# Moving the last of seven block products behind the next pair's second one, and three repeated weight loads some steps later

## The chip, the cores and the metric

One Trainium2 chip, one of its cores. The metric is device time in microseconds (us) of one execution of the whole kernel, taken as the median over runs. Engines are named as the profile names them: PE is TensorE, DVE is VectorE, ACT is ScalarE, POOL is GpSimd, SP is SyncE, which here issues DMAs.

## The reference, cut to what matters

The kernel computes one encoder layer over 1024 tokens of width 1024. A normed input goes through one combined projection into windowed attention, a two-way RWKV-7 scan and gates; their sum is projected and added to `x`. Behind that come the two steps that the change touches, and a gated embedding:

```python
hf = rms_norm(x, norm_ffn[i])
x = x + jnp.square(jax.nn.relu(hf @ w_ff1[i])) @ w_ff2[i]
hp = rms_norm(x, norm_ple[i])
x = x + (p[i] @ w_ple[i]) * jax.nn.sigmoid(hp @ w_ple_gate[i])
```

`w_ff1` is 1024 x 4096 and `w_ff2` 4096 x 1024, all in 32-bit floats. `hf @ w_ff1` is called the first MLP product here, the product with `w_ff2` the second.

## The kernel before, in words

Every operand of a matmul is split in two: ACT casts it to a rounded high part (line 187), DVE or POOL subtracts to get the low part (line 188). A product of two operands is then three matmuls, high x high, high x low and low x high, accumulated in a PSUM bank.

Both MLP products are done as 2 x 2 blocks with seven block products instead of eight, the sums and differences of blocks being formed on DVE.

**First MLP product** (lines 1300 to 1555). The 4096 hidden columns are 32 blocks of 128; pair `p` of 16 (`NPR`) takes blocks `p` and `p + 16`. Its raw weights come in two loads of 512 KB, one for each block (`w1_load`, line 1315), into the tile `w1st`, which has one buffer. From them `w1_op(p, r)` makes the operand of block product `r`: for S1 to S4 first sums on DVE (lines 1324 to 1331, tile `ssum`), then the split into `w1h` and `w1l`. Each of the seven operands has one buffer of its own, so `w1_op(p + 1, r)` must wait for product `r` of pair `p`. The right-hand sides are the normed tokens and their sums, made once: `fh`/`fl` (for A11 and A12), `rh`/`rl` (S2 and S4), `T1`, `T3` and `T4` (S1, S3, A22).

`product` (line 1442) is one block product: 12 matmuls of 128x512 into one bank of a pool of six (`ff1ps`). A pair takes three banks. `pa` gets A11 and then A12 on top; `pb` gets S2, then S3, then A22; `pc_` gets S1, then S4. Between them the partial sums are read out: line 1475 copies A11 (`c1`), line 1518 adds `c1` and `pb` after S2 (`u2`), line 1522 copies `pc_` after S1 (`c5`), line 1531 adds `c1` and `pb` after S3 (`u3`), line 1537 adds after S4, line 1547 after A22. Since S3 and A22 are added to what stands in `pb`, each must wait until the read before it is done. `relu2` squares the positive part, on ACT (lines 1457 and 1458) or, for A12's result, on DVE (line 1460). `hsum` (line 1465) forms the sums that the second product needs, and `put` (line 1469) stores the seven hidden blocks of a pair to DRAM, 256 KB each.

The loop of line 1495 runs over pairs. It is written in the order A11, S2, S1, A12, S3, S4, A22, and behind each product `then(r)` prepares the same operand of the next pair. The load for the pair after the next is written at the end. Pairs 0 and 1 have their A11 and A12 done ahead of the loop, and are interleaved in part.

**Second MLP product** (lines 1560 to 1720). Seven block products again (`PRODS`), each of 16 steps `p`; a step takes one hidden block (`hid_d`, tile `sst`, left side, split into `sh` and `sl`) and one block of `w_ff2` or a sum of such blocks (split into `th` and `tl`), and does 12 matmuls into four banks. B11's 16 blocks are kept raw in `b11`, since later products need them for sums. In the first block product, steps 0 to 2 (`NPRE`) take operands that were loaded and split during the first MLP product (`pre`); for these B11 is loaded a second time, into `b11` (line 1681). Steps 3 and on load B11 into `b11` (line 1606) and split it from there. From step 8 on (`T1EARLY` is 8) `t1_of(0)`, `t1_of(1)` and so on form T1 = B12 - B11 beside the products; they are the first to read the repeated blocks.

A scheduler orders the instructions of each engine, by dependencies and priority, at build time; each engine then runs its own in that order. SP's DMAs are one such queue: an issue that waits for a buffer holds up the issues behind it.

Of the kernel before, what the change touches and what calls it, by code (L numbers as in the profile page):

```python
# [12 lines left out]
ALU = mybir.AluOpType  # L13
# [124 lines left out]
def block_kernel(ctx: ExitStack, tc: tile.TileContext, I: dict, out: bass.AP):  # L138
    nc = tc.nc

    def pool(stack, name, bufs=1, **kw):
        return stack.enter_context(tc.tile_pool(name=name, bufs=bufs, reuse_waits="tile", **kw))
# [333 lines left out]
    with ExitStack() as s1:  # L476
# [75 lines left out]
        s2 = A1.tile([P, 2, 512], F32R, name="s2")  # L552
# [61 lines left out]
        for p in range(NP):  # L614
# [24 lines left out]
            for d in range(ND):  # L639
# [8 lines left out]
                if d == 0:  # L648
                    nc.vector.memset(E[:, :, 0:1], 1.0)
                    E1, E2, last = E[:, :, 0:C], E[:, :, 1:C + 1], C - 1  # L650
                else:
                    nc.vector.memset(E[:, :, C:C + 1], 1.0)
                    E1, E2, last = E[:, :, 1:C + 1], E[:, :, 0:C], 0
# [151 lines left out]
    with ExitStack() as s2:  # L805
# [16 lines left out]
        for n in range(NT):  # L822
# [6 lines left out]
            for kv in range(2):  # L829
# [6 lines left out]
                for h in range(4):  # L836
                    sc = PA.tile([P, nk * P], F32, name="sc", tag="sc", bufs=2)
                    for j in range(2):
                        nc.tensor.matmul(sc, qT[:, 4 * kv + h, :], kT[:, kv, j, k0 * P:k1 * P], start=(j == 0), stop=(j == 1))
                    nc.vector.tensor_tensor_reduce(  # L840
                        out=sm[:, h, 0:nk * P], in0=sc, in1=band[:, b0:b0 + nk, :].rearrange("p b t -> p (b t)"), scale=1.0,
# [460 lines left out]
    NPR = FF // P // 2  # L1302
# [136 lines left out]
    def bank():  # L1439
        return PG.tile([P, 512], F32, name="ff1ps", tag="w", bufs=6)  # L1440

    def product(ps, p, r, start=True):

        ah, al = wop[p, r]
        bh, bl = right[SUMS[r]]
        for k in range(4):
            for i, (x_, y_) in enumerate(((ah, bh), (ah, bl), (al, bh))):
                nc.tensor.matmul(ps, x_[:, k, :], y_[:, k, :], start=start and k + i == 0, stop=k == 3 and i == 2, skip_group_check=True)  # L1448

    def tmp(name, bufs=1):  # L1450
        return FP.tile([P, 512], F32, name=name, bufs=bufs)

    def relu2(src_, on_act):

        h = tmp("h", 7)
        if on_act:
            nc.scalar.activation(out=h, in_=src_, func=AF.Relu)  # L1457
            nc.scalar.activation(out=h, in_=h, func=AF.Square)  # L1458
        else:
            nc.vector.scalar_tensor_tensor(out=h, in0=src_, scalar=0.0, in1=src_, op0=ALU.max, op1=ALU.mult)  # L1460
        return h

    def hsum(a_, b_, op):
        h = tmp("h", 7)
        nc.vector.tensor_tensor(out=h, in0=a_, in1=b_, op=op)  # L1465
        return h

    def put(p, r, h):
        nc.sync.dma_start(hid_d[r][p], h)
# [8 lines left out]
    for p in range(2):  # L1478
        pa, pb = bank(), bank()
# [12 lines left out]
    sFP = ExitStack()  # L1492
    FP = pool(sFP, "post", side="right")
    sRF = ExitStack()
    for p in range(NPR):
        def then(r):

            if p + 1 < NPR:
                w1_op(p + 1, r)

        if p == 1:
            w1_op(2, "A11")
            w1_op(2, "A12")
        if p > 1:
            pa = bank()
            product(pa, p, "A11")
            c1_of(p, pa)
            then("A11")
        else:
            s_ = tmp("u2")  # L1510
            nc.vector.tensor_tensor(out=s_, in0=c1s[p], in1=first[p], op=ALU.add)
            a11 = relu2(s_, True)
            put(p, "A11", a11)
        pb, pc_ = bank(), bank()
        c1 = c1s[p]
        product(pb, p, "S2")
        u2 = tmp("u2")
        nc.vector.tensor_tensor(out=u2, in0=c1, in1=pb, op=ALU.add)
        then("S2")
        product(pc_, p, "S1")  # L1520
        c5 = tmp("c5")
        nc.scalar.copy(c5, pc_)
        then("S1")
        if p > 1:
            product(pa, p, "A12", start=False)
            a11 = relu2(pa, True)
            put(p, "A11", a11)
            then("A12")
        product(pb, p, "S3", start=False)
        u3 = tmp("u3")  # L1530
        nc.vector.tensor_tensor(out=u3, in0=c1, in1=pb, op=ALU.add)
        nc.vector.tensor_tensor(out=c5, in0=c5, in1=u3, op=ALU.add)
        a22 = relu2(c5, True)
        put(p, "A22", a22)
        then("S3")
        product(pc_, p, "S4", start=False)
        nc.vector.tensor_tensor(out=u2, in0=u2, in1=pc_, op=ALU.add)
        a21 = relu2(u2, True)
        s1 = hsum(a21, a22, ALU.add)
        put(p, "S1", s1)  # L1540
        s2 = hsum(s1, a11, ALU.subtract)
        put(p, "S2", s2)
        put(p, "S3", hsum(a11, a21, ALU.subtract))
        then("S4")
        product(pb, p, "A22", start=False)
        u3 = tmp("u3")
        nc.vector.tensor_tensor(out=u3, in0=c1, in1=pb, op=ALU.add)
        a12 = relu2(u3, False)
        put(p, "A12", a12)
        put(p, "S4", hsum(a12, s2, ALU.subtract))  # L1550
        then("A22")
        if p + 2 < NPR:
            w1_load(p + 2)
        if p == NPR - 2:
            RF = pool(sRF, "ff2a", bufs=1, side="right")
# [6 lines left out]
    NPRE, NR2, T1EARLY = 3, 5, 8  # L1562

    def w2_block(p, b):
        f, n = p + NPR * (int(b[1]) - 1), int(b[2]) - 1
        return w2[f * P:(f + 1) * P, 512 * n:512 * n + 512]
# [23 lines left out]
    b11 = pool(sB11, "b11").tile([P, NPR, 512], F32, name="b11r")  # L1590
# [84 lines left out]
    for ip, (lr_, rr_, bs, fresh) in enumerate(PRODS):  # L1675
        if fresh:
            banks[bs] = [acc() for _ in range(4)]
        for p in range(NPR):
            if ip == 0 and p < NPRE:
                sh, sl, th_, tl_ = pre[p]  # L1680
                nc.sync.dma_start(b11[:, p], w2_block(p, "B11"))
            else:
                sh, sl = parts_of(F2, ("sh", "sl"), fetch(F2, hid_d[lr_][p], "sst", 3), NR2)
                th_, tl_ = parts_of(F2, ("th", "tl"), right_of(p, rr_), NR2)
            for i in range(4):
                isl = slice(i * P, (i + 1) * P)
                for j, (x_, y_) in enumerate(((sh, th_), (sh, tl_), (sl, th_))):
                    nc.tensor.matmul(banks[bs][i], x_[:, isl], y_, start=fresh and p + j == 0,  # L1688
                                     stop=p == NPR - 1 and j == 2, skip_group_check=True)
            if ip == 0 and p == NPRE - 1:  # L1690
                sRF.close()
                sFP.close()
                PXX = pool(sX, "x1", side="right")
                X = [PXX.tile([P, 4, DM], F32, name=f"X{e}") for e in range(2)]
                c1 = pool(sC1, "c1", side="right").tile([P, 4, 512], F32, name="c1r")
                t2r = pool(sT2, "t2", side="right").tile([P, NPR, 512], F32, name="t2r")
                t1r = pool(sT1, "t1", side="right").tile([P, NPR, 512], F32, name="t1r")
            if ip == 0 and p >= NPR - T1EARLY:
                t1_of(p - (NPR - T1EARLY))
            if ip == 1 and p % 2 == 0:  # L1700
                e, i = divmod(p // 2, 4)
                t = torder[4 * e + i]
                nc.sync.dma_start(X[e][:, i, :], x1_d[t * P:(t + 1) * P, :])
            if ip == 3 and p < 12:
                add_to(*((0, 1), (1, 1), (1, 0))[p // 4], p % 4, c1[:, p % 4])
            if ip > 3 and p % 3 == 1:
                load_next()
            if ip == 6:
                if p == 4:
                    pt, xs = ple_load(0), ple_norm(0)  # L1710
                    ple_scale(0, *xs)
                if p == 9:
                    nxt = [ple_p(pt), ple_x(xs[0])]
        for i in range(4):
            b_ = banks[bs][i]
            if ip == 0:
                nc.scalar.copy(c1[:, i], b_)
            else:
                for e, n in {1: [(0, 1)], 2: [(0, 0)], 3: [(1, 1)], 4: [(1, 1)], 5: [(1, 0)], 6: [(0, 1)]}[ip]:
                    add_to(e, n, i, b_)  # L1720
        if ip == 3:
            sB11.close()
            PLEW = pool(sP, "plew")
            gainp = PLEW.tile([P, DM], F32, name="gainp", bufs=1)
            nc.sync.dma_start(gainp, I["gains"][2:3, :].partition_broadcast(P))
            wp = [PLEW.tile([P, 2, DM], F32R, name=f"wp{i}", bufs=1) for i in range(2)]
            loads += [(wp[0][:, k:k + 1], wp[1][:, k:k + 1], wpv[:, k:k + 1]) for k in range(2)]
            ple_gate_w(PLEW, 0)
        if ip == 4:
            sT1.close()  # L1730
            PLEW2 = pool(sP, "plew2")
            ple_gate_w(PLEW2, 1)
            ple_gate_w(PLEW2, 2)
        if ip == 5:
            sT2.close()
            PLEW3 = pool(sP, "plew3")
            ple_gate_w(PLEW3, 3)
            PXS = pool(sT2, "plex", bufs=2, side="right")
# [64 lines left out]
```

## Time and profile before

| what | value |
|---|---|
| median of 3 runs | 1830.6 us (1830.04 to 1831.61) |
| profiled execution, its own time | 1829.44 us |
| its span, first to last instruction | 1827.7 us |
| granted TensorE clock, mean | 0.977 |
| DMA | 285.96 MB, 156 GB/s in the mean |

In the rows that the prediction shows, a row of the timeline has start, duration, engine, line, operation and tiles, and in brackets the idle time of the engine before it and what ended that. A row of a window has the stretch, its length, the busy time of each engine with the count of instructions (all five engines, or only PE and its weight loads where asked for one line), the granted clock, the DMA share and GB/s. `PEld` is the weight load, which overlaps the matmuls; `SPq` is SP's queue of DMA issues. Tile names are shown without buffer numbers: `ff1ps` is any bank of the first product, `u` is `u2` or `u3`.

### The profile page before, as it was taken

The numbers are of one execution on the slowest core, as the hardware profiler recorded it, in microseconds if no ns is written. First come the engines' busy times: TensorE is split into PE (matmuls) and PEld (weight loads), VectorE is DVE, ScalarE is ACT, GpSimd is POOL, SyncE is SP. The second block draws the span as 40 slices with busy tenths as digits, with TensorE's granted clock in tenths as the row PEclk, the third lists the DMA queues.
The fourth block names the chain that finished last, engine by engine and source line by source line (L and its number), as shares of the span: only waits on it lengthen the run. The fifth ranks groups of instructions, "written<-read, shape, count | busy, mean of one in ns | idle before, by whom it ended". The sixth has DMA issues, their size and how long they took to land. (4 is left out here: it accounts for less than half of the span.)

```text
span 1827.7 us, 29641 instructions
## 1 busy us (share of the span) xinstructions
PE 1718.2 (94%) x11288; PEld 1376.0 (75%) x11288; DVE 1132.3 (62%) x1931; ACT 879.1 (48%) x1624; POOL 320.2 (18%) x265
## 2 busy tenths in 40 slices
PE   7999888999999898988889989999999999999998
PEld 7976666666677777766668867787887888888887
DVE  5646777745935656676464387666665877685442
ACT  5536666547754555456532255444444444554321
POOL 3454544532132121112132000000000000000000
PEclk9999999989999999999899989999999999999999
DMA  6362444674377474576565305544445974574111
GB/s 202 99 176 73 124 144 144 196 204 115 102 202 202 141 196 139 170 208 199 178 211 175 104 35 162 171 146 133 158 154 208 318 251 127 190 219 136 61 41 46
DMA packets 281998, 285.96 MB, mean 156 GB/s; under 512 B 49408, under 2 KB 195712, under 8 KB 281728
## 3 DMA queue, kind: packets, MB, share of 16 engines
q1 hardware_dynamic: 273600, 270.76, 48.1%
q0 software_dynamic: 7824, 12.59, 2.5%
q8 instruction: 89, 1.46, 0.3%
q10 hardware_dynamic: 432, 0.73, 0.1%
q14 instruction: 53, 0.43, 0.1%
HBM read 203.26 MB, written 80.74 MB: 155 GB/s over the span
## 5 line engine op out<-in xcount | busy, mean ns | idle before, releaser
L188 POOL TENSOR_TENSOR wlo<-wst,whi 128x512 fp32r<-128x512 f32 x100 | 149.5, 1507 | 318.7 <-ACT whi L187 263.3
L1688 PE MATMUL ff2ps<-th,sh 128*128 128x512 f32 x448 | 173.7, 390 | 2.9 <-ACT th L187 2.9
L1688 PE MATMUL ff2ps<-tl,sh 128*128 128x512 f32 x448 | 174.3, 389 | 0.0
L1688 PE MATMUL ff2ps<-th,sl 128*128 128x512 f32 x448 | 174.3, 389 | 0.0
L175 POOL TENSOR_TENSOR rstd<-ms,neghalf 128x1 f32<-128x1 f32 x24 | 13.2, 553 | 803.4 <-DVE ms L173 803.4
L187 ACT CAST sh<-sst 128x512 fp32r<-128x512 f32 x109 | 67.8, 622 | 116.3 <-PE ff2ps L1688 71.7
L188 DVE TENSOR_TENSOR sl<-sst,sh 128x512 fp32r<-128x512 f32 x109 | 75.1, 689 | 54.1 <-ACT sh L187 53.7
L1688 PEld LDWEIGHTS ff2ps<-th,sh 128*128 128x128 f32 x448 | 83.9, 188 | 21.1 <-ACT th L187 3.6
L1688 PEld LDWEIGHTS ff2ps<-tl,sh 128*128 128x128 f32 x448 | 84.1, 188 | 17.5 <-DVE tl L188 0.2
L1688 PEld LDWEIGHTS ff2ps<-th,sl 128*128 128x128 f32 x448 | 84.1, 188 | 17.5
L187 ACT CAST whi<-wst 128x512 fp32r<-128x512 f32 x100 | 60.7, 618 | 51.1 <-DMA wst<-in_w_in_dram 17.7
L187 ACT CAST w1h<-w1st 128x512 fp32r<-128x512 f32 x48 | 29.1, 614 | 104.4 <-DMA w1st<-in_w_ff_dram 102.9
L188 DVE TENSOR_TENSOR w1l<-w1st,w1h 128x512 fp32r<-128x512 f32 x48 | 32.7, 687 | 57.3 <-ACT w1h L187 57.3
L208 PE MATMUL gps<-rm,bkp 128*128 128x256 f32 x256 | 62.4, 386 | 1.5 <-DVE Z L752 1.0
L1034 DVE TENSOR_TENSOR gm<-gps,gmask 128x512 f32<-128x512 f32 x64 | 43.7, 685 | 29.9 <-PE gps L208 29.9
L218 PE MATMUL gmm<-hh,wlo 128*128 128x512 f32 x144 | 58.9, 409 | 0.0
L216 PE MATMUL gmm<-hl,whi 128*128 128x512 f32 x144 | 58.9, 409 | 0.0
L214 PE MATMUL gmm<-hh,whi 128*128 128x512 f32 x144 | 58.8, 408 | 0.0
L187 ACT CAST w1h<-ssum 128x512 fp32r<-128x512 f32 x64 | 39.4, 615 | 35.9 <-DVE ssum L1324 23.8
L208 PEld LDWEIGHTS gps<-rm,bkp 128*128 128x128 f32 x256 | 47.5, 190 | 11.0 <-issue 1.5
L1086 DVE COPY Wt<-wps 64x512 f32<-64x512 f32 x16 | 10.9, 679 | 71.5 <-PE wps L208 71.5
L226 PE MATMUL mm<-hh,whi 128*128 128x512 f32 x128 | 51.4, 401 | 4.0 <-ACT z L520 4.0
(409 smaller groups left out, 5058.0 us busy)
## 6 DMA issues: line engine op xcount, KB each, us to landing
wst<-in_w_in_dram SPq DMA_DIRECT2D x92, 256.0 KB, 3.5
tst<-in_w_ff_dram SPq DMA_DIRECT2D x80, 256.0 KB, 3.9
w1st<-in_w_ff_dram SPq DMA_DIRECT2D x32, 512.0 KB, 5.5
hid_S<-h SPq DMA_DIRECT2D x64, 256.0 KB, 2.1
sst<-hid_S SPq DMA_DIRECT2D x64, 256.0 KB, 2.7
hid_A<-h SPq DMA_DIRECT2D x48, 256.0 KB, 2.0
sst<-hid_A SPq DMA_DIRECT2D x45, 256.0 KB, 3.7
ra_d<-ra SPq DMA_DIRECT2D x8, 1024.0 KB, 4.5
```

The costliest lines, as they stand in the source:

```text
L175: nc.gpsimd.tensor_tensor(out=r, in0=ms, in1=neghalf.broadcast_to([P, width]), op=ALU.pow)
L187: a = nc.scalar.copy(hi, src)
L188: b = (lo_eng or nc.vector).tensor_tensor(out=lo, in0=src, in1=hi.bitcast(F32), op=ALU.subtract)
L208: tc.keep_in_program_order(nc.tensor.matmul(*a, **kw))
L214: mm(ps, ah, bh, start=(i == 0), stop=False)
L216: mm(ps, ah, bl, start=False, stop=False)
L218: mm(ps, al, bh, start=False, stop=(i == n - 1))
L226: nc.tensor.matmul(ps, ah, bh, start=(i == 0), stop=False)
L1034: nc.vector.tensor_tensor(out=gm[d][:, s % NB, 4 * h:4 * h + 4, :], in0=ps.rearrange("p j q t -> p (j q) t"), in1=gmask[:, d, :].unsqueeze ...
L1086: nc.vector.tensor_copy(Wt[own[0], 0], wp[own[0]])
L1688: nc.tensor.matmul(banks[bs][i], x_[:, isl], y_, start=fresh and p + j == 0, stop=p == NPR - 1 and j == 2, skip_group_check=True)
```

## The change

```diff
+    def last_product(p, pb, c1, s2):
+
+        product(pb, p, "A22", start=False)
+        u3 = tmp("u3")
+        nc.vector.tensor_tensor(out=u3, in0=c1, in1=pb, op=ALU.add)
+        a12 = relu2(u3, False)
+        put(p, "A12", a12)
+        put(p, "S4", hsum(a12, s2, ALU.subtract))
+        if p + 1 < NPR:
+            w1_op(p + 1, "A22")
+
+    last = None
     for p in range(NPR):
...
         then("S2")
+        if last:
+            last_product(*last)
         product(pc_, p, "S1")
...
         then("S4")
-        product(pb, p, "A22", start=False)
-        u3 = tmp("u3")
-        nc.vector.tensor_tensor(out=u3, in0=c1, in1=pb, op=ALU.add)
-        a12 = relu2(u3, False)
-        put(p, "A12", a12)
-        put(p, "S4", hsum(a12, s2, ALU.subtract))
-        then("A22")
+        last = (p, pb, c1, s2)
+        if p == NPR - 1:
+            last_product(*last)
         if p + 2 < NPR:
             w1_load(p + 2)
...
                 sh, sl, th_, tl_ = pre[p]
-                nc.sync.dma_start(b11[:, p], w2_block(p, "B11"))
...
+            if ip == 0 and 0 <= p - (NPR - T1EARLY - NPRE) < NPRE:
+                q = p - (NPR - T1EARLY - NPRE)
+                nc.sync.dma_start(b11[:, q], w2_block(q, "B11"))
             if ip == 0 and p >= NPR - T1EARLY:
                 t1_of(p - (NPR - T1EARLY))
```

In the first part the A22 product of a pair, with the add, the squaring, the two stores and the preparation of the next A22 operand that belong to it, moves from the end of its pair to behind S2 of the next pair; the last pair's stays. In the second part the repeated loads of B11's blocks 0 to 2 move from steps 0 to 2 to steps 5 to 7 of the second product's first block product. No operation is added or taken out.

PE in a middle pair, where A22 stood (before): the last matmuls of S4 in one bank, and then A22 (right side `T4`) in `pb` of the same pair.

```order
L1448 MATMUL ff1ps_11394<-rl_10583,w1h_11343 128x512
L1448 MATMUL ff1ps_11394<-rh_10582,w1l_11344 128x512
L1448 MATMUL ff1ps_11393<-T4h_10588,w1h_11367 128x512
L1448 MATMUL ff1ps_11393<-T4l_10589,w1h_11367 128x512
L1448 MATMUL ff1ps_11393<-T4h_10588,w1l_11368 128x512
```

PE, where A22 stands now: behind the last matmuls of the next pair's S2 (bank `ff1ps_11533`).

```order
L1448 MATMUL ff1ps_11533<-rl_10583,w1h_11389 128x512
L1448 MATMUL ff1ps_11533<-rh_10582,w1l_11390 128x512
L1448 MATMUL ff1ps_11369<-T4h_10588,w1h_11413 128x512
L1448 MATMUL ff1ps_11369<-T4l_10589,w1h_11413 128x512
L1448 MATMUL ff1ps_11369<-T4h_10588,w1l_11414 128x512
```

Between S3 into a bank and A22 into it there now stand S4 of the same pair and A11 and S2 of the next.

DVE in a middle pair, before: from the split of the A22 operand, the last reader of the raw tile `w1st_11207`, to the add after S3 (line 1531).

```order
L188 TENSOR_TENSOR w1l_11368<-w1st_11207,w1h_11367 128x512
L1465 TENSOR_TENSOR h_11364<-h_11361,h_11335 128x512
L1518 TENSOR_TENSOR u2_11407<-c1_11387,ff1ps_11393 128x512
L188 TENSOR_TENSOR w1l_11390<-w1st_11371,w1h_11389 128x512
L1324 TENSOR_TENSOR ssum_11409<-w1st_11371 128x512
L1325 TENSOR_TENSOR ssum_11410<-ssum_11409,w1st_11371 128x512
L188 TENSOR_TENSOR w1l_11452<-w1st_11371,w1h_11451 128x512
L188 TENSOR_TENSOR w1l_11432<-ssum_11409,w1h_11431 128x512
L188 TENSOR_TENSOR w1l_11414<-ssum_11410,w1h_11413 128x512
L1328 TENSOR_TENSOR ssum_11474<-w1st_11371 128x512
L1531 TENSOR_TENSOR u3_11467<-c1_11387,ff1ps_11393 128x512
```

DVE in the same place now: line 1500 is the add after A22 of the pair before, line 1546 the add after S3.

```order
L1500 TENSOR_TENSOR u3_11405<-c1_11199,ff1ps_11205 128x512
L188 TENSOR_TENSOR w1l_11414<-w1st_11183,w1h_11413 128x512
L1460 SCALAR_TENSOR_TENSOR h_11407<-u3_11405 128x512
L1465 TENSOR_TENSOR h_11410<-h_11407,h_11335 128x512
L188 TENSOR_TENSOR w1l_11366<-w1st_11347,w1h_11365 128x512
L188 TENSOR_TENSOR w1l_11452<-w1st_11347,w1h_11451 128x512
L1324 TENSOR_TENSOR ssum_11385<-w1st_11347 128x512
L1325 TENSOR_TENSOR ssum_11386<-ssum_11385,w1st_11347 128x512
L1328 TENSOR_TENSOR ssum_11474<-w1st_11347 128x512
L188 TENSOR_TENSOR w1l_11432<-ssum_11385,w1h_11431 128x512
L188 TENSOR_TENSOR w1l_11390<-ssum_11386,w1h_11389 128x512
L1546 TENSOR_TENSOR u3_11467<-c1_11363,ff1ps_11369 128x512
```

The split of the A22 operand, on which the next load of `w1st` waits, has moved behind the add of line 1500 and so behind the moved product; the add after S3 still stands behind the splits and sums of the newly loaded raw tile.

SP's queue at the start of the second product, before: the stores of the last pair, and among them the loads into `b11` (line 1681 the repeated ones, line 1606 those of steps 3 and on).

```order
L1681 DMA b11r_13353<-in_w_ff2_dram 128x512
L1469 DMA hid_A12_70<-h_13297 128x512
L1469 DMA hid_S4_75<-h_13300 128x512
L1681 DMA b11r_13353<-in_w_ff2_dram 128x512 x2
L1606 DMA b11r_13353<-in_w_ff2_dram 128x512 x3
L1575 DMA sst_13485<-hid_A11_69 128x512
L1606 DMA b11r_13353<-in_w_ff2_dram 128x512
```

SP's queue there now: line 1617 is the load of steps 3 and on, line 1710 a repeated load.

```order
L1617 DMA b11r_13353<-in_w_ff2_dram 128x512
L1469 DMA hid_A12_70<-h_13297 128x512
L1469 DMA hid_S4_75<-h_13300 128x512
L1617 DMA b11r_13353<-in_w_ff2_dram 128x512 x2
L1710 DMA b11r_13353<-in_w_ff2_dram 128x512
L1586 DMA sst_13483<-hid_A11_69 128x512
L1617 DMA b11r_13353<-in_w_ff2_dram 128x512
L1710 DMA b11r_13353<-in_w_ff2_dram 128x512
```

Step 3's block has taken the place of the first repeated load, and the repeated ones stand one each behind the blocks of steps 5, 6 and 7.

## The prediction

> **What bounds the kernel now.** The page comes first: how full is the busiest engine, and does anything queue up in front of it?
>
> ```profile
> span 1827.7 us, 29641 instructions
> PE 1718.2 (94%) x11288; PEld 1376.0 (75%) x11288; DVE 1132.3 (62%) x1931; ACT 879.1 (48%) x1624; POOL 320.2 (18%) x265
> L1688 PE MATMUL ff2ps<-th,sh 128*128 128x512 f32 x448 | 173.7, 390 | 2.9 <-ACT th L187 2.9
> ```
>
> TensorE (PE) is busy for 94% of the span; the DMA queues, VectorE (DVE) and ScalarE (ACT) are far from full. What can be won by moving work is PE idle time, and the change touches two stretches of it: the waits inside the first MLP product, and the single wait of 2.9 us in the second (last row). For the first, the view of PE's waits, asked over the first product (us in total, times, longest):
>
> ```profile
> PE ff1ps L1448 <- DVE u L1531: 6.1, 8, 1.9
> PE ff1ps L1448 <- ACT w1h L187: 1.5, 1, 1.5
> PE ff1ps L1448 <- ACT c L1522: 0.7, 1, 0.7
> PE ff1ps L1448 <- DVE w1l L188: 0.6, 1, 0.6
> ```
>
> Eight of the waits end with one instruction, the add of line 1531, which reads the bank `pb` after S3; A22 writes the same bank next, so it must wait. That view counts idle gaps of the engine as modelled. What the waits cost in pace is read from the view of windows, matmuls of line 1448 alone:
>
> ```profile
> 1125.84:1396.10 270.26, 264.10 (x1153) 215.17 (x1151) 1.00 0.46 149
> 1264.87:1267.59 2.72, 2.72 (x14) 2.25 (x13) 1.00 0.85 207
> ```
>
> The second row is one block product without a wait: 12 matmuls start to start in 2.72 us. The first row runs from product S1 of pair 2 (pairs count from 0) to the end of the last pair: 5 products of pair 2 and 7 of each of 13 pairs, 96 in all. 96 x 2.72 = 261.1 us, so 270.26 - 261.1 = 9.1 us of the stretch are waits and their restarts. The timeline of one pair shows where they come from:
>
> ```profile
> 1259.43 0.39 PE L1448 MATMUL ff1ps<-fh,w1h 128*128 128x512 f32 x1
> ...
> 1262.15 0.39 PE L1448 MATMUL ff1ps<-rh,w1h 128*128 128x512 f32 x1
> ...
> 1263.66 0.69 DVE L188 TENSOR_TENSOR w1l<-w1st,w1h 128x512 fp32r<-128x512 f32 x1
> ...
> 1264.38 0.38 SPq L1315 DMA_DIRECT2D w1st<-in_w_ff_dram  x1
> ...
> 1265.56 0.42 SPq L1315 DMA_DIRECT2D w1st<-in_w_ff_dram  x1
> ...
> 1269.06 0.62 ACT L187 CAST w1h<-w1st 128x512 fp32r<-128x512 f32 x1 [6.13 <-DMA w1st<-in_w_ff_dram]
> ...
> 1269.71 0.69 DVE L188 TENSOR_TENSOR w1l<-w1st,w1h 128x512 fp32r<-128x512 f32 x1 [3.89 <-ACT w1h L187]
> ...
> 1271.30 0.69 DVE L1324 TENSOR_TENSOR ssum<-w1st 128x512 f32<-128x512 f32 x1 [0.89 <-DMA w1st<-in_w_ff_dram]
> ...
> 1273.03 0.39 PE L1448 MATMUL ff1ps<-rh,w1h 128*128 128x512 f32 x1
> ...
> 1273.24 1.29 DVE L188 TENSOR_TENSOR w1l<-ssum,w1h 128x512 fp32r<-128x512 f32 x2
> ...
> 1275.65 0.68 DVE L1531 TENSOR_TENSOR u<-c,ff1ps 128x512 f32<-128x512 f32 x1
> ...
> 1276.38 0.50 PE L1448 MATMUL ff1ps<-T4h,w1h 128*128 128x512 f32 x1 [0.47 <-DVE u L1531]
> ```
>
> A11 starts at 1259.43 and S2 at 1262.15; S4 starts at 1273.03, when S3 is done. The add 1531 could run then, but starts at 1275.65: DVE runs in order, and in front of the add stand the splits of the next pair's weights, which were held up by their load (3.89 and 0.89 us of DVE idleness, ended by way of the load). S4 covers 2.72 us of that; the rest PE pays at A22 (1276.38).
>
> **First part: A22 behind the next pair's S2.** Same matmuls, same adds, same DMAs; only places change. The new order of a steady pair on PE, from the start of its A11 as 0: A11 to 2.7, S2 to 5.4, A22 of the pair before to 8.2, S1 to 10.9, A12 to 13.6, S3 to 16.3, S4 to 19.05. The add after S3 now has until 24.5 (S2 of the next pair done) before A22 needs the bank. It can be as late as in the rows above, 2.6 us after S3, and still lie hidden by three products, 8.2 us. All waits on line 1531 go. The last pair keeps its old order, but has no next weights to split, and shows no wait now.
>
> What is late next is the weights. The raw tile `w1st` has one buffer, and its last reader is the split of a pair's A22 weights, which must wait until the A22 product of the pair before has released the operand tile. So the load for the next pair comes behind the moved product: 8.2, cast 0.62, split 0.69, issue at 9.6 and about 10.2. Before, it came at 4.95 and 6.1 (1264.38 and 1265.56 less 1259.43). From issue to use took 1269.06 - 1264.38 = 4.7 us and 1271.30 - 1265.56 = 5.7 us, so the halves are there at 14.3 and 15.9. Behind them DVE has two splits, three sums and the splits of S1 and S2; with ACT's first cast and 0.65 us per operation (two took 1.29) that is 14.9 + 7 x 0.65 = 19.5. S2 of the next pair needs its weights at 19.05 + 2.72 = 21.8: 2.3 us to spare. A11's split is done by 15.6 and needed at 19.05. So I put the steady state at no wait: -9.1 us, if every wait of the stretch goes.
>
> [...]
>
> The start is tighter, since pairs 0 and 1 are interleaved:
>
> ```profile
> 1109.44 0.62 ACT L187 CAST th<-st 128x512 fp32r<-128x512 f32 x1 [2.35 <-DMA st<-in_w_ff_dram]
> 1110.33 0.38 SPq L1315 DMA_DIRECT2D w1st<-in_w_ff_dram  x1
> ...
> 1112.09 0.50 PE L1448 MATMUL ff1ps<-rh,w1h 128*128 128x512 f32 x1 [0.68 <-ACT c L1522]
> ```
>
> In the new order A22 of pair 0 is followed by 11 matmuls of S1 of pair 1; those end, as now, at 1112.09 - 0.68 = 1111.4, so A22 ends 2.5 us earlier, at 1108.9. ACT still waits for `th` (to 1110.1), squares, then casts A22 of pair 1 (to 1111.1); DVE splits it by 1112.1. The load of pair 2 so starts 1.8 us later than 1110.33 and is used from 1116.8; cast to 1117.4. PE at 1111.4 has S3 and S4 left, and wants A11 of pair 2 at 1116.8: about 0.6 us of wait, and as much again for S2's weights. Against that, the wait on line 1522 goes, since S3 now stands there. Without waits S1 of pair 2 would start at 1111.4 + 5 x 2.72 = 1125.0; with them at 1126.2; before it was 1125.84. I take +0.4 us; bounds -0.9 (no new wait) and +3 (the load 2.6 us slower).
>
> The moved puts of A12 and S4 now stand behind the two weight loads on SP's queue and go out at about 10, when their values are made; nobody reads them before the second product. `pb` is held until about 9 in the next pair; with six banks and three per pair it is wanted again only in the pair after that. The price is nothing.
>
> **Second part: the repeated B11 loads.** The start of the second product:
>
> ```profile
> 1398.55 0.33 SPq L1681 DMA_DIRECT2D b11r<-in_w_ff_dram  x1
> ...
> 1401.06 0.91 SPq L1681 DMA_DIRECT2D b11r<-in_w_ff_dram  x2
> ...
> 1402.01 1.46 SPq L1606 DMA_DIRECT2D b11r<-in_w_ff_dram  x3
> ...
> 1404.08 0.39 PE L1688 MATMUL ff2ps<-th,sl 128*128 128x512 f32 x1
> ...
> 1406.66 1.94 ACT L187 CAST th<-b11r 128x512 fp32r<-128x512 f32 x3 [7.73 <-DMA b11r<-in_w_ff_dram]
> ...
> 1407.33 0.97 PE L1688 MATMUL ff2ps<-th,sh 128*128 128x512 f32 x3 [2.86 <-ACT th L187]
> ...
> 1409.50 0.62 ACT L187 CAST th<-b11r 128x512 fp32r<-128x512 f32 x1 [0.26 <-DMA b11r<-in_w_ff_dram]
> ```
>
> The three loads of line 1681 fetch blocks already split; line 1606 fetches step 3's, which PE waits for. Now step 3's load takes the first of these places, at 1398.55. The DMA view, asked over that issue alone, and two windows:
>
> ```profile
> b11r<-in_w_ff_dram SPq DMA_DIRECT2D x1, 256.0 KB, 3.6
> 1404.20:1407.20 3.00, 0.27 (x2) 0.00 (x0) 0.00 (x0) 0.54 (x1) 0.00 (x0) 1.00 0.95 340
> 1440.00:1483.00 43.00, 43.00 (x191) 35.60 (x190) 36.48 (x59) 19.55 (x35) 0.00 (x0) 1.00 0.91 299
> ```
>
> It lands at 1398.55 + 3.6 = 1402.2, is cast by 1402.8 and split by 1403.5. PE's next matmul would be due at 1404.08 + 0.23 = 1404.3 and came at 1407.33: -3.0 us. Bounds: 0, if the bytes only move the wait, and -3.0, since nothing more is idle there. The moved loads now stand among steps 6 to 8. Step 6's block has five loads ahead of it instead of seven, step 8's eleven as before. Step 6 was split about 1410.8 (cast at 1409.50) and PE, 3.0 us sooner, reaches it at 1404.3 + 3 x 2.72 = 1412.5: covered. Further on the queues carry the same bytes at a share of 0.91 while PE is full, and the loads there wait for PE to free their buffers, so they move with it.
>
> **Sum.** -9.1 + 0.4 - 3.0 = -11.7 us. The profiled execution took 1829.44 us (span 1827.7 and 1.7 around it) and would take 1817.7; the median of the runs is 1830.6, so I forecast 1818.9 us. A measurement of this kernel tells about 0.2%, 3.7 us, from no change.
>
> **Rivals.**
> A, the wait comes back in part as weights. DVE idles for the load and then has seven operations in a row, now over 4 us later in the pair. If S2's weights come 2.7 us later than I work out, PE waits 0.4 us in each of 13 pairs: 1818.9 + 5.2 = 1824.1. For: clearance is only 2.3 us. Against: landings of 4.7 and 5.7 us, and the second half now follows the first directly.
> B, the second stall only moves to steps 4 to 8: 1818.9 + 3.0 = 1821.9. For: the DMA share of 0.95. Against: the places counted above.
> C, the other side: the load is the new bound. With one buffer, A22, load, sums, splits and S2 are a loop that must close within 19.05 us. It decides where the loads take over 2.3 us longer than the rows; from 2.3 + 11.7 / 13 = 3.2 us longer the gain is gone. At 4 us longer, 13 x 1.7 = 22 us: 1841. For: the chain has no second buffer. Against: no row here shows an extra 3 us. Long waits could also cost clock:
>
> ```profile
> 1084.00:1088.00 4.00, 4.00 (x10) 3.05 (x10) 4.00 (x8) 2.15 (x3) 0.00 (x0) 0.50 0.00 0
> ```
>
> Here, just behind PE's idle time in the stage before, the granted clock was 0.50: 10 matmuls in 4 us. In the row at 1404.20 an idle 2.9 us left it at 1.00. [...]
> D, the order changes, but A22 then waits as long for something else at its new place, such as its own weights: only the second part is left, 1830.6 - 3.0 = 1827.6, not to be told from no change. Against: by the reckoning above A22's weights are split at 9.6 of their own pair, 15 us before the product.
>
> **How the numbers follow.** Forecast 0.74, A 0.11, B 0.06, C 0.04, D 0.05. The range holds the forecast, B and A: from 1816.8 (start term at -0.9, and a little for timed runs that wait more than the profiled one) to 1824.8. Faster: forecast, A and B, 0.91. Same: D, 0.05. Slower: C, 0.04.
>
> **What would show it.** Right: no wait of PE on the add after S3; the stretch from S1 of pair 2 to the second product within 262 us; the load issued 9 to 10 us into a pair; step 3's cast near its load's landing and PE without a gap there. Wrong: PE waits ended by `w1l`, `w1h` or `w1st` in every pair (A, C), by A22's own weights (D), or by `th` or `tl` in steps 4 to 8 (B).

## The result, and the profile after

| | median of the runs | range, runs |
|---|---|---|
| before, same chip | 1831.11 us | 1827.38 to 1833.3, 6 |
| after | 1818.02 us | 1813.7 to 1822.48, 6 |

The ratio is 0.993, with a 95% interval of 0.9913 to 0.9948: 12.8 us faster, between 9.5 and 15.9. The forecast was 1818.9. The profiled execution took 1818.63 us, its span is 1816.9.

First the page of the changed kernel: the span, the engines, and the group of matmuls that waited for step 3's block before (its line is now 1698).

```profile
span 1816.9 us, 29645 instructions
PE 1714.2 (94%) x11288; PEld 1376.5 (76%) x11288; DVE 1135.8 (63%) x1931; ACT 883.1 (49%) x1624; POOL 321.7 (18%) x265
L1698 PE MATMUL ff2ps<-th,sh 128*128 128x512 f32 x448 | 173.9, 389 | 0.0
```

The work is the same, and the 2.9 us of idle time in front of that group are 0.0. Next the view of PE's waits over the first product and the start of the second, matmuls of line 1448:

```profile
PE ff1ps L1448 <- ACT w1h L187: 1.7, 2, 1.5
PE ff1ps L1448 <- DVE w1l L188: 0.6, 1, 0.6
```

Both rows were there before, with 0.2 us less in the first; the row of the add after S3 (6.1 us in 8 waits) and the row of line 1522 (0.7 us) are gone. The view of windows, line 1448 alone, from S1 of pair 2 to the second product:

```profile
1126.95:1388.07 261.12, 261.12 (x1153) 216.03 (x1151) 1.00 0.46 152
```

261.12 us is 96 times 2.72 us: there is no wait left in this stretch, which took 270.26 us before. One steady pair in the timeline, its A11 starting at 1252.07:

```profile
1259.32 0.39 PE L1448 MATMUL ff1ps<-T4h,w1l 128*128 128x512 f32 x1
...
1260.20 0.62 ACT L187 CAST w1h<-w1st 128x512 fp32r<-128x512 f32 x1 [2.94 <-PE ff1ps L1448]
...
1261.03 0.69 DVE L188 TENSOR_TENSOR w1l<-w1st,w1h 128x512 fp32r<-128x512 f32 x1
...
1261.74 1.01 SPq L1315 DMA_DIRECT2D w1st<-in_w_ff_dram  x2
...
1266.02 1.15 ACT L187 CAST w1h<-w1st 128x512 fp32r<-128x512 f32 x2 [2.29 <-DMA w1st<-in_w_ff_dram]
1266.68 1.30 DVE L188 TENSOR_TENSOR w1l<-w1st,w1h 128x512 fp32r<-128x512 f32 x2 [3.63 <-ACT w1h L187]
...
1268.39 0.39 PE L1448 MATMUL ff1ps<-rh,w1h 128*128 128x512 f32 x1
...
1269.82 1.29 DVE L188 TENSOR_TENSOR w1l<-ssum,w1h 128x512 fp32r<-128x512 f32 x2
...
1271.03 0.68 DVE L1546 TENSOR_TENSOR u<-c,ff1ps 128x512 f32<-128x512 f32 x1
...
1273.83 0.39 PE L1448 MATMUL ff1ps<-rh,w1h 128*128 128x512 f32 x1
...
1276.55 0.39 PE L1448 MATMUL ff1ps<-T4h,w1h 128*128 128x512 f32 x1
```

VectorE is still idle for the load, for 3.63 us. The add after S3 (now line 1546) still comes late: S4 starts at 1268.39, the add at 1271.03, 2.64 us later. But nobody waits for it: its reader A22 starts at 1276.55. The weights of S2, which starts at 1273.83, are split at 1269.82 + 1.29 = 1271.11, 2.7 us ahead.

The start of the second product, loads and operands:

```profile
1390.18 0.33 SPq L1617 DMA_DIRECT2D b11r<-in_w_ff_dram  x1
...
1393.90 0.62 ACT L187 CAST th<-b11r 128x512 fp32r<-128x512 f32 x1 [2.27 <-DMA b11r<-in_w_ff_dram]
1393.98 0.45 SPq L1710 DMA_DIRECT2D b11r<-in_w_ff_dram  x1
...
1394.56 0.69 DVE L188 TENSOR_TENSOR tl<-b11r,th 128x512 fp32r<-128x512 f32 x1 [1.33 <-ACT th L187]
...
1397.40 1.23 ACT L187 CAST th<-b11r 128x512 fp32r<-128x512 f32 x2 [2.87 <-DMA b11r<-in_w_ff_dram]
```

Step 3's block is asked for at 1390.18 and split at 1395.25; the product starts at 1388.07, so PE needs it at 1388.07 + 3 x 2.72 = 1396.2.

### The profile page after: what moved, and what is told of

Its sections match the earlier page's. It is cut to its first block, busy times and chain, and to the rows that moved or that the text cites. A ratio compares the mean times of both kernels' runs of the same rounds, so it can differ in the third digit from the quotient of the medians.

```text
span 1816.9 us, 29645 instructions
## 1 busy us (share of the span) xinstructions
PE 1714.2 (94%) x11288; PEld 1376.5 (76%) x11288; DVE 1135.8 (63%) x1931; ACT 883.1 (49%) x1624; POOL 321.7 (18%) x265
## 5 line engine op out<-in xcount | busy, mean ns | idle before, releaser
L188 DVE TENSOR_TENSOR w1l<-ssum,w1h 128x512 fp32r<-128x512 f32 x64 | 43.0, 688 | 16.9 <-ACT w1h L187 16.9
```

Source lines behind the costliest of these rows:

```text
L188: b = (lo_eng or nc.vector).tensor_tensor(out=lo, in0=src, in1=hi.bitcast(F32), op=ALU.subtract)
```

## The experiments

Times of whole executions scatter here by more than these effects: those of the kernel before run from 1824.7 to 1843.1 us over the chips used. The traces show where. The first matmul of line 1448 starts anywhere between 1057.6 and 1079.7 us, while the two products behind it repeat to within 1.6 us. So the experiments are read first by three lengths from the traces, start to start of matmuls in us: the 96 products from S1 of pair 2 on, the second product from its first matmul to its last, and both products whole.

| kernel | first product starts | 96 products | second product | both |
|---|---|---|---|---|
| before | 1066.55 | 270.26 | 311.09 | 640.64 |
| before, again | 1065.54 | 270.17 | 312.90 | 642.20 |
| after | 1066.86 | 261.12 | 308.32 | 629.52 |
| after, again | 1079.73 | 261.12 | 307.93 | 628.11 |
| first part alone | 1065.74 | 261.12 | 314.60 | 634.57 |
| first part alone, again | 1067.41 | 261.12 | 313.51 | 634.22 |
| second part alone | 1057.61 | 270.47 | 309.51 | 639.97 |
| A22 one product earlier | 1071.46 | 261.12 | 307.93 | 627.72 |
| A22 one product earlier, again | 1058.65 | 261.73 | 307.89 | 627.76 |
| A22 one product later | 1071.07 | 265.28 | 307.94 | 632.72 |
| no weight loads | 1064.36 | 261.12 | 312.98 | 632.28 |
| first half loaded twice | 1063.56 | 275.15 | 307.90 | 642.04 |
| repeated loads left out | 1068.16 | 261.12 | 308.96 | 631.10 |

**The theory**: in the kernel before, a load of W1 held VectorE's queue, the queue held the add after S3, and the add held A22; the change takes the add off PE's path and does nothing to the queue. The second stall is a load that stood behind three others. **The rivals** are those of the prediction: weights late instead (A, C), the second stall moved (B), or another wait for A22 (D).

**The first part alone.** Edit against the changed kernel:

```
+                nc.sync.dma_start(b11[:, p], w2_block(p, "B11"))    # steps 0 to 2
...
-            if ip == 0 and 0 <= p - (NPR - T1EARLY - NPRE) < NPRE:
-                q = p - (NPR - T1EARLY - NPRE)
-                nc.sync.dma_start(b11[:, q], w2_block(q, "B11"))
```

> The moved A22 product alone; the repeated B11 loads stay at steps 0 to 2, ahead of step 3's. Theory (the waits on the add after S3 and the stall at step 3 are separate, and only what ends them counts): all waits on that add go, the stretch from S1 of pair 2 to the second product keeps its 261 to 262 us, the stall at step 3 stays at 2.9 to 3.0 us, and the time is 8.7 to 9.0 us under the kernel before, 3.0 us over the changed kernel. Rival 1 (the two parts lean on each other: the stall at step 3 came from the first product ending late or early): the stall is not 3 us here and the gain is under 7 or over 10.5 us. Rival 2 (the gain of the first part is in truth smaller and the rest is due to the second part): under 6 us.

Median 1821.43 us of 7 runs against 1834.04 of 19, ratio 0.993 (0.9904 to 0.9956): the times cannot tell it from the changed kernel. The trace can. The 96 products take 261.12 us, 9.14 less than before, as expected. But the stall at step 3 is 3.62 us, and what comes behind it costs more:

```profile
1394.49:1397.69 3.20, 0.00 (x1) 0.01 (x1) 0.02 (x1) 0.62 (x1) 0.00 (x0) 0.89 1.00 351
1397.69:1401.69 4.00, 4.00 (x9) 3.14 (x10) 3.97 (x6) 3.71 (x6) 0.00 (x0) 0.50 1.05 389
1401.69:1405.69 4.00, 4.00 (x15) 3.19 (x14) 2.63 (x5) 1.15 (x3) 0.00 (x0) 0.74 0.94 324
```

These are windows over all lines; the first number in brackets counts the matmuls, the third from the end is the granted clock. It falls to 0.50 behind the idle time: 9 matmuls in 4 us, where the kernel before has 17 in the 4 us behind its stall, at a clock of 1.00. The second product takes 314.60 us, 6.3 more than in the changed kernel. So the expectation failed in its last term: this kernel is 5.1 us behind the changed one in the two products (634.57 against 629.52) instead of 3.0. By the letter this is the sign of rival 1, a stall of over 3 us and a gain of under 7 (640.64 - 634.57 = 6.1 us). The first product gained its full 9.14; why the stall was longer is taken up below, with the repeated loads.

**The second part alone.** The same move of the three loads, made in the kernel before.

> The moved loads alone; A22 stays in its own pair. Theory: PE's wait for step 3's block (2.86 us in the profile before) is gone, no wait of over 0.5 us stands in steps 4 to 8, the waits on the add after S3 are all still there; 3.0 us under the kernel before, about 9 us over the changed kernel. Rival 1 (the bytes only move the wait): 0 us, with a wait on th or tl of 2 to 3 us among steps 4 to 8. Rival 2 (the loads matter elsewhere too): over 4.5 us.

The ratio is 0.9971 (0.9952 to 0.999), that is 5.3 us less, between 1.8 and 8.8 (12 runs, median 1829.5). In the trace the stall of step 3 is gone, and three short waits are new:

```profile
PE ff1ps L1448 <- DVE u L1531: 6.4, 9, 1.7
...
PE ff2ps L1687 <- DVE tl L188: 0.7, 3, 0.2
```

The waits on the add after S3 are all there (first row), so the parts are separate. The 0.7 us stand at 1399.69, 1468.23 and 1474.20, none over 0.24: rival 1, that the wait only moves by 2 to 3 us, is out. The interval of the times holds the 3.0 us of the theory and the over 4.5 of rival 2 alike; the traces have to decide. The trace's second product is 1.6 us shorter than the first trace of before, 3.4 shorter than the second one.

**A22 one product earlier and one later.** The call of `last_product` stands behind the next pair's A11, or behind its S1, instead of behind its S2:

```
         ...                       # A11 of this pair
+        if last: last_product(*last)      # earlier
         ...                       # S2
-        if last: last_product(*last)      # the changed kernel
         ...                       # S1
+        if last: last_product(*last)      # later
```

> The changed kernel with the last product of the pair before one place earlier: behind the next pair's A11, ahead of its S2. Theory: the add after S3 has 5.4 us of cover instead of 8.2, and was 3.2 us behind S3's end in the changed kernel's trace, so it is still covered; the load of the next weights goes out 2.7 us earlier, S2's weights have about 5.4 us to spare instead of 2.7. Neither decides: the same time as the changed kernel within 1.5 us, less by up to 0.5 us if the start of pair 2 no longer waits. Rival 1 (what counts is how late the weights' load goes out: an earlier load hinders the add again): waits on the add come back, 3 us or more slower than the changed kernel. Rival 2 (the changed kernel still pays for late weights): 2 us or more faster than the changed kernel.

> The changed kernel with the last product of the pair before one place later: behind the next pair's S1, so that PE's order is A11, S2, S1, A22 of the pair before. Theory: the load goes out 2.7 us later in each pair; the changed kernel's trace has S2's weights 2.7 us ahead of their use, so that margin is used up: 0 to 0.4 us of wait in each of 13 pairs, at w1l or w1h in front of S2, 0 to 5 us slower than the changed kernel, and still some 7 us or more under the kernel before. Rival 1 (the load has more room than worked out, since DVE has less queued ahead of it later in the pair): no change, under 0.5 us, and no waits on w1l. Rival 2 (the load loop is steep: a late load also slows the ones behind it): over 8 us slower than the changed kernel.

Earlier: 261.12 us again, no wait on the add; ratio 0.9889 (0.9855 to 0.9923). Later: 265.28 us, 4.2 us more than the changed kernel, ratio 0.9928 (0.99 to 0.9955). PE's waits of the later place, from 1100 us to the second product:

```profile
PE ff1ps L1448 <- ACT w1h L187: 2.2, 2, 1.5
PE ff1ps L1448 <- DVE w1l L188: 0.8, 3, 0.3
```

The second row is new (the changed kernel's 0.6 us of that name stand ahead of 1100 us): S2 waits for its weights. With the restarts and the waits too short for this view that is 0.32 us in each of 13 pairs, inside the 0 to 0.4 expected. The margin of 2.7 us in the changed kernel is real, and one more product uses it up. Rival A of the prediction is this kernel: it names the right wait, at a place that the change doesn't reach.

**Both once more, side by side on one chip.**

> The changed kernel once more, unaltered, beside the next one on the same chip. Theory: first and second product together, from the first matmul of line 1448 to the last of line 1698, take 629 to 630 us as in its first trace (640.6 in the kernel before), and the time is 11 to 13 us under the kernel before; what differs from run to run lies ahead of the first product. Rival (the first trace was a lucky one): over 632 us for the two products, or waits on the add after S3.

> The changed kernel with the last product of the pair before behind the next pair's A11, once more, beside the changed kernel. In its first trace the two products took 627.7 us, 1.8 us less than in the changed kernel; 0.7 us of that are the waits at the start of pair 2, the rest stretches at half clock and one short wait. Theory: 0.5 to 2 us under the changed kernel in the traces, too little to tell from the times alone. Rival (the earlier place is worth more, as the first times had it, 0.989 against 0.993): 4 us or more under the changed kernel.

The changed kernel: 1819.17 us, ratio 0.9928 (0.9905 to 0.9951), 628.11 us for the two products. Its profiled execution took 1830.12 us, since its first product started 12.9 us later than in the first trace, at 1079.73; 628.11 us is a little under the expected 629 to 630. One product earlier: 1813.18 us, ratio 0.9909 (0.9882 to 0.9937), 627.76 us. Its 96 products take 261.73 us, since one wait of 0.31 us on the add after S3 came back, in pair 3: the smaller cover was not always enough. The medians differ by 6 us, but the traces give the earlier place 0.35 us here (0.5 to 2 were expected) and 1.8 us in the first pair of traces, and the intervals overlap. A version that beats the changed kernel by more than that is not shown.

**The first part alone, once more.** The same kernel as in the first experiment.

> The first part alone, once more, for one look. In its first trace step 3 of the second product waited 3.62 us and the 15 matmuls behind it started 0.427 us apart instead of 0.227. Theory (the wait is a landing time, which varies, and it is the length of the idle time that sets the clock off): the wait is between 2.8 and 3.8 us; where it is near 2.9 us as in the kernel before, no matmul behind it is slowed; where it is near 3.6 us, the same 14 to 16 matmuls are, for 2.9 us more. Rival 1 (the longer wait belongs to the moved product): 3.5 to 3.8 us again. Rival 2 (the slow stretch has another cause than the wait): slowed matmuls behind a wait of under 3 us, or none behind 3.6 us.

```profile
1400.45:1404.45 4.00, 4.00 (x11) 3.23 (x12) 3.96 (x6) 3.71 (x6) 0.00 (x0) 0.62 1.00 359
1404.45:1408.45 4.00, 4.00 (x19) 3.31 (x18) 3.02 (x6) 2.20 (x5) 0.00 (x0) 1.00 0.88 318
```

These windows stand behind a wait of 3.97 us. The wait is over what the theory and rival 1 allowed (3.8 us). Slowed matmuls stand behind it again, so rival 2 is out, but only 8 of them, for 1.5 us instead of 2.9: how long the slow stretch lasts does not follow the wait's length alone.

**No weight loads.** In the kernel before, pairs 2 to 15 take pair 1's raw weights:

```
+        if p > 1:
+            wraw[p] = wraw[1]
+            return
```

> The kernel before with the weight loads of pairs 2 to 15 of the first product left out: those pairs take pair 1's raw weights again (their values are replaced by pair 1's); casts, splits, sums and adds stay, A22 stays in its own pair. Theory (the add after S3 was late because VectorE's queue stood behind splits that waited for a load): with no load to wait for, the waits on the add are gone or under 1 us in total, and the stretch from S1 of pair 2 to the second product takes 261 to 262 us instead of 270.3. Rival (VectorE has too many operations ahead of the add, load or not): at least 4 us of waits on the add are left. Step 3's wait in the second product is not touched by either.

The window of line 1451 (line 1448 of the other kernels) from S1 of pair 2 on:

```profile
1122.54:1383.66 261.12, 261.12 (x1153) 216.03 (x1151) 1.00 0.27 98
```

261.12 us with A22 in its old place. VectorE does the same operations as before; without the load it is early enough. So the load, by way of VectorE's queue, is the cause, and the amount of VectorE's work is not.

**The kernel before, once more.**

> The kernel before, unaltered, once more for one look. Its first trace had a wait of 2.86 us at step 3 of the second product and full clock behind it; the two traces of the first part alone, which has the same loads in the same places, had 3.62 and 3.97 us and matmuls 0.427 us apart behind it, and so had the trace without weight loads, with 3.15 us. Theory (the wait's length varies with the landing, and the first trace happened to stay short of what sets the clock off): 2.8 to 4 us here, and slowed matmuls behind it if it is over 3.1 us. Rival (in the order of before it is always near 2.9 us, and the longer ones belong to the first product ending without waits): 2.8 to 3.0 us, full clock. Either way the stretch from S1 of pair 2 to the second product takes 270 to 271 us.

Its stall at step 3 is 3.09 us, and the clock falls behind it, just under the 3.1 us from which slowed matmuls were expected. The 96 products take 270.17 us, as expected. More telling is one of the waits among them, in the timeline:

```profile
1233.26 0.39 PE L1448 MATMUL ff1ps<-rh,w1l 128*128 128x512 f32 x1
1235.64 0.50 PE L1448 MATMUL ff1ps<-T4h,w1h 128*128 128x512 f32 x1 [1.99 <-DVE u L1531]
...
1237.29 0.63 PE L1448 MATMUL ff1ps<-T4h,w1h 128*128 128x512 f32 x1
1237.71 0.63 PE L1448 MATMUL ff1ps<-T4l,w1h 128*128 128x512 f32 x1
```

And two windows, all lines, clock again third from the end. The first holds the whole wait:

```profile
1233.58:1236.99 3.41, 1.42 (x7) 1.11 (x7) 3.41 (x7) 1.20 (x3) 0.00 (x0) 1.00 0.21 77
1236.99:1240.40 3.41, 3.41 (x10) 2.65 (x9) 1.78 (x4) 3.25 (x6) 0.00 (x0) 0.50 0.21 77
```

A wait of 1.99 us; six matmuls started at a clock of 1.00; then 3.41 us at half clock, which costs 1.6 us. In the first trace a wait of 1.87 us at the same place left no mark. So a wait of 1.99 us was followed by half clock here, and the 2.86 us at step 3 of the first trace was not.

The records of the granted clock show what went with it. The half-clock stretches at 1236.99 and 1407.65 here start 170.66 us apart, 50 times 3.413 us, and last 3.41 us each. In the first trace of before and the first of after, the half-clock stretches (18 and 13, without the last of the kernel) start whole multiples of 3.413 us apart and last one to three times that. Cut at these starts into steps of 3.413 us, the two products have 184 and 180 steps at full clock. In one step of each trace, at the start of the first product, PE is without a matmul for 2.62 and 2.29 us, and half clock follows; in the other 362 it is 1.74 us at most, and none is followed by half clock. A wait that falls across two steps is divided: the 2.86 us of the first trace of before left 1.12 us in one and 1.74 in the next (first two rows, the step and the one behind it, both at 1.00), the 3.09 us here 1.03 and 2.06, and half clock behind that (last two rows). Ahead of the first product the same reading does not separate the steps: 1.61 us (before, from 886.76) was followed by half clock, 1.88 us (after, from 932.89) was not. All of this is read off these traces; no run set the place of a wait among the steps.

```profile
1405.59:1409.00 3.41, 1.67 (x7) 1.30 (x8) 1.67 (x3) 2.23 (x4) 0.00 (x0) 1.00 1.03 376
1409.00:1412.41 3.41, 3.41 (x17) 2.79 (x16) 3.13 (x6) 2.85 (x6) 0.00 (x0) 1.00 1.07 400
1404.24:1407.65 3.41, 1.35 (x6) 1.02 (x7) 1.24 (x2) 1.81 (x3) 0.00 (x0) 1.00 1.00 364
1407.65:1411.06 3.41, 3.41 (x10) 2.65 (x9) 3.40 (x6) 3.07 (x6) 0.00 (x0) 0.50 1.04 395
```

**The price of a late load.** In the changed kernel, from pair 3 on:

```
+        if p > 2:      # behind both halves
+            nc.sync.dma_start(st[:, 0], w1v[:, :, p * P:(p + 1) * P])
```

> The changed kernel with a third load per pair from pair 3 on: the first half of the raw weights is fetched a second time behind both halves (the same bytes to the same place), so that the operands of a pair are made some microseconds later. This puts a price on the load loop as the bound, the side on which the change would have lost. Theory (A22, load, sums, splits and S2 are a loop that must close within 19.05 us, with 2.7 us to spare in the changed kernel's trace): the repeat waits for the first landing and takes another 4 to 5 us, S2's weights come 1.2 to 2.2 us late, every one of 13 pairs waits, 16 to 29 us slower than the changed kernel, that is slower than the kernel before. Rival 1 (the loop has far more slack than worked out, or the repeat lands with the second half): under 5 us slower. Rival 2 (long waits also cost clock): over 40 us, with stretches of matmuls 0.427 us apart in each pair.

Median 1834.34 us over nine executions against 1831.41, ratio 1.0016 (0.9999 to 1.0034): the gain is gone. (A tenth execution took 3357.61 us; it is in neither number, and its cause is not known.) The stretch takes 275.15 us, 14.0 more than in the changed kernel, or 1.08 us in each of 13 pairs. That is a little less than the 16 to 29 expected, and it is another operand that is late:

```profile
1245.55 1.01 SPq L1315 DMA_DIRECT2D w1st<-in_w_ff_dram  x2
1249.86 0.37 SPq L1317 DMA_DIRECT2D w1st<-in_w_ff_dram  x1
1251.50 0.69 DVE L1326 TENSOR_TENSOR ssum<-w1st 128x512 f32<-128x512 f32 x1 [4.66 <-DMA w1st<-in_w_ff_dram]
...
1254.57 1.14 ACT L187 CAST w1h<-w1st 128x512 fp32r<-128x512 f32 x2 [1.72 <-DMA w1st<-in_w_ff_dram]
```

The pair's A11 started at 1235.44, so the repeat's bytes are used 19.1 us into the pair, 5.2 us later than the 13.95 in the changed kernel. VectorE meanwhile makes the sum that needs the second half alone (line 1326), and no wait on S2's weights shows. A11's weights are late: cast at 13.95 + 0.62 = 14.6 in the changed kernel, needed at 19.05, they had 4.5 us to spare, and 5.2 - 4.5 = 0.7 us is what is missing in this pair. The next A11 starts at 1255.24, 19.8 us behind this one instead of 19.05; the mean over 13 pairs is the 1.08. No half clock follows: the granted clock of the stretch is 1.00, and the waits are 1.0 us at most.

**The repeated loads left out.** Instead of them, at step 5:

```
+                nc.gpsimd.memset(b11[:, 0:NPRE], 0.0)
```

> The changed kernel with the three repeated B11 loads left out (those three blocks are set to zero instead, by GpSimd at step 5, so that the last sums that use them are of other values). Theory (at steps 5 to 7 these loads cost nothing): the second product takes 307.9 to 308.3 us as in the changed kernel's traces. Rival (they still cost something at the new place, hidden in short waits): 307.9 us against 308.3 us at most, that is no more than 0.4 us, or, if they delayed the loads of steps 6 to 12, a wait of the changed kernel that is gone here.

308.96 us for the second product, 0.6 us more than the longer of the changed kernel's two traces. Two short waits on `tl` (0.23 and 0.09 us) and part of a pace loss behind one of them are all that is found. Leaving the loads out gains nothing, so at their new place they cost nothing that can be seen; what the memset adds is not separated from that. This trace also has the longest wait at the start of pair 2, 1.1 us for A11's weights.

## Why the prediction was right, step by step

**The waits on the add, -9.1 us.** Right in mechanism and size: -9.14 us in the first trace, and 261.12 us in both traces of the changed kernel. The chain of causes holds too: take the load away and the waits go without the move; make the move and the add is as late as before (2.64 us behind S3, 2.6 foreseen) and nothing waits.

**The weights behind the moved product.** The schedule held to half a microsecond. Counted from A11: issue 9.67 us (9.6 foreseen), first half cast from 13.95 (14.3), S2's weights split at 19.04 (19.5), PE there at 21.76 (21.8). The clearance is 2.7 us where 2.3 was foreseen. The landing agrees with the rows of before, 4.7 us from issue to use for the first half: the DMA view of the pair shown above has 4.8 us from issue to landing (last number):

```profile
w1st<-in_w_ff_dram SPq DMA_DIRECT2D x2, 512.0 KB, 4.8
```

**The start, +0.4 us.** Its waits came (0.20, 0.16 and 0.34 us at A11 and S2 of pair 2 in the first trace of after, with part of their pace loss), and the wait of line 1522 (0.84 with its pace loss) went. From the last wait that both orders share (it ends at 1097.52 us before and 1098.49 after) to S1 of pair 2 the stretch took 28.32 us before and 28.46 after: +0.1 us. In the other traces with A22 behind the next pair's S2 it took 28.32 to 28.44, and 29.50 in one (the last experiment). It lies in the bounds. What the first trace lost before pair 2, 0.8 us in all, is mostly the half-clock stretch at the start of the first product, which ended 23.0 us into the product instead of 21.6 and which no edit touches.

**The repeated loads, -3.0 us.** Right for the profiled execution: 311.09 to 308.32 us is -2.8. But the bound was wrong. The prediction put "-3.0, since nothing more is idle there" as the most that could be won. The stall is a landing time; it was 2.86, 3.09, 3.15, 3.62 and 3.97 us in five traces with the old order of loads, and in four of them the clock fell behind it. The load's removal from PE's path so won 2.8 to 6.7 us (second product 311.09 to 314.60 with the stall, 307.93 to 308.32 in the changed kernel). Step 3's block was asked for 5.9 us into the second product in all five and cast 4.65, 4.88, 4.93, 5.42 and 5.77 us after that, so the whole difference lies between issue and landing. What decides how long a landing takes is open: the stall was over 3.1 us in the three traces whose 96 products had no waits and under it in the two of before, which is too few to tell.

**The sum.** -9.14 in the 96 products, +0.79 ahead of them and -2.77 in the second product make -11.1 us in the first pair of traces, against -11.7. Over two traces of each kernel the two products take 641.4 and 628.8 us, -12.6, beside the 12.8 of the times. That the median after came within 0.9 us of the forecast is in part luck: single executions of the changed kernel lie up to 8.8 us apart.

**The rivals.** A, B and D found nothing in the steady pairs or in steps 4 to 8 of the trace to stand on. C's place was right, its point was not reached; with the first half used 5.2 us later, the gain is gone. In its remark on the clock, the row in which 2.9 us left the clock at 1.00 does not show that such gaps are safe. Waits of 1.99 and 3.09 us in the second trace of before were followed by half clock. The 2.9 us had been divided between two of the 3.413 us steps, 1.74 us at most in one.

## What to carry to other kernels

When an engine waits for a late operation that stands in another engine's queue behind a load, it can be enough to move the reader: put independent work between, and count how far the move pushes the next load, because that is the side on which it can lose. The margin of such a loop is worth measuring by moving one step too far; here one product further cost 0.3 us a pair. Where whole times scatter, compare the stretches that the edit touches, and take a second trace of the kernel before ahead of setting bounds from one wait.

## What was not expected of the hardware

- **Half clock followed a wait of 1.99 us.** Behind waits of 1.99, 3.09, 3.15, 3.62 and 3.97 us the matmuls came 0.427 us apart instead of 0.227, for about 3 to 6 us, which cost 1.4 to 2.9 us each; behind 1.87 and 2.86 us they did not. Counted within the 3.413 us steps read off the traces, the idle time in the two products was 2.62, 2.29, 2.06 and 1.99 us in four steps that half clock followed (first traces of before and after, second of before), and 1.74 us at most in the 362 full-clock steps of the first two traces that it did not follow. No run varied that time by itself. The slow stretch can begin well after the restart: its first matmul starts 1.65 us later in the timeline above.
- **The stage ahead sets the scatter.** The first product started between 1057.61 and 1079.73 us over 13 traces of kernels whose code is the same up to there. Most of that goes with time at half clock: the mean granted clock was 0.983 over the 1818.1 us of the earliest trace (the second part alone) and 0.971 over the 1828.3 us of the latest (the changed kernel again). What the mean is short of 1, taken as time lost, is an estimated 31 and 53 us, 22 us apart as the two starts are. The first traces of before and after, with 71.7 us at half clock ahead of the first product in each, start it within 0.31 us of each other. Why the executions differ in it was not tried.
